# A latent output product with four units of seven products in place of three, and the residual's loads ten ticks later

## The chip, the core and the metric

The kernel runs on one NeuronCore of a Trainium2 chip. The core has a matrix engine (PE, with PEld for its weight loads), a vector engine (DVE), a scalar engine (ACT), a general engine (POOL) and a synchronisation engine (SP); each works through its own list of instructions in a fixed order. SP and POOL issue the DMAs that bring data from memory; the DMAs of both share the core's 16 DMA engines. The metric is the device time of one execution in microseconds (us), the median of several runs; lower is better.

## The reference

One layer of a decoder with 256 tokens and a model width of 2048: two attention branches (a latent one, A, and a sliding-window one, B), each with a gate, merged and put through W_out, then a gated feed-forward part with a short convolution. The place that matters is the output product of branch A, `o_a @ w_o_mla`, a 256 x 2048 by 2048 x 2048 product:

```python
    o_a = mla_attention(q[..., :MLA_NOPE_DIM], q_rope, kv[..., :MLA_NOPE_DIM], k_rope, kv[..., MLA_NOPE_DIM:])
    o_b = swa_attention(q_s, k_s, v_s, swa_sinks, rel_table)
    g = jax.nn.sigmoid(gates.astype(jnp.float32)).reshape(B, S, N_BRANCHES, D_MODEL)
    merged = g[:, :, 0] * (o_a @ w_o_mla).astype(jnp.float32) + g[:, :, 1] * (o_b @ w_o_swa).astype(jnp.float32)
    return merged.astype(h.dtype) @ w_out
...
        y = hybrid_mixer(h, w_in[l], mla_q_norm[l], mla_w_q_up[l], mla_kv_norm[l], mla_w_kv_up[l],
                         swa_sinks[l], rel_bias_table, w_o_mla[l], w_o_swa[l], w_out[l])
        x = x + rms_norm(y, norm_mix_post[l])
```

## The kernel before

**Products in three passes.** All weights are float32. A chunk of weights (128 x 1024, 512 KB) is loaded into a raw buffer; ACT rounds it to a high part `whi` (line 164), DVE subtracts that from the raw chunk and keeps the rest as a low part `wlo` (line 165). Each product is then three matmuls, high by high, high activations by low weights, and low by high (`mm3`, lines 199 to 201). So a chunk goes through load (SP), cast (ACT), subtraction (DVE), matmuls (PE).

**The A pair.** `a_pair` (line 1079) computes the first 1024 of the 2048 output columns of `o_a @ w_o_mla` with `pair_gemm` (line 274). The inner dimension is cut into eight units of two 128-row blocks. A plain unit ("p", line 288) takes two chunks, each with 4 products, that is 12 matmuls, so 24 in all. A unit of seven products ("s", line 301) is a Strassen-like step on 2 x 2 blocks with 7 products, that is 21 matmuls, but it takes four chunks: row block 2u+1 (2 products), the first half of row block 2u (1 product, a load of 256 KB), and two "parked" chunks `tw{u}_0` and `tw{u}_1` (2 products each) that hold differences of weight blocks. It needs sums of the activations too: `a_sums` (line 1060) makes them on DVE with one cast on ACT (`token_sums`, line 376) into the tiles `as0` (units 0 and 1) and `as1` (units 2 and 3). `A_ORDER` says which unit follows which; the seven-product units are the units 0, 1, 2 ... in turn, the plain ones the rest.

**Parking.** The differences in `tw{u}_*` are made long before, in the attention stage, by `park_sums` (line 238): POOL loads two 512 KB chunks into the single tile `tw{u}_s`, DVE does four subtractions of 128 x 512 (line 253), POOL stores two 512 KB results to memory. One more such job, `tc0` for a later product, comes after them and uses the same single tile.

**Buffers.** `RING = 4` pairs of `whi`/`wlo` and `RAW = 3` raw buffers are used in turn. Within the A pair four more raw buffers are in the rotation: chunk by chunk it goes raw, flex, raw, half of `araw`, raw, flex, other half of `araw` (line 1086), with two flex buffers. A load may be issued only when the DVE subtraction of the chunk that last had its buffer is over, and a cast may start only when PE is done with the chunk four before. After the A pair comes the product for columns 1024 to 1535, an ordinary `gemm` (line 203) of eight chunks, c0 to c7 in what follows, 12 matmuls each, with the raw buffers in the order raw, raw, flex, flex, raw.

**What else runs there.** At the end of the pair's last seven-product unit DVE combines the sums into `uda` (lines 356 to 361), adds the plain part (line 1094) and merges with the gates (lines 1069 and 1070). `late_loads` (line 1026) issues eight SP loads of 256 KB that bring the residual x into `x2_0` and `x2_1`; these tiles lie where `as0` and `as1` were, so they wait for PE's last use of the sums. `w_place` (line 1178) later takes the space of `araw` for two POOL loads of W_out, `mr` (512 KB each, lines 326 and 327): they are issued once the last chunk in `araw` has been subtracted.

**Order.** `at(t, f)` puts a step at a due time in ticks (a unit of either kind is two ticks, a chunk of an ordinary product one). The framework's scheduler makes each engine's final order from that program order and the dependences, so a due time is a wish, and the resulting lists are what counts.

Of the kernel before, what the change touches and what calls it, by code (L numbers as in the profile page):

```python
# [42 lines left out]
def trunk_layer(ctx, tc, x, x_cols_in, conv_cols_in, g_mix_post, g_ffn_post, w_in, w_q, w_kv,  # L43
# [16 lines left out]
    def sb(pl, shape, name, dt=F32, tag=None, bufs=None):  # L60
        return pl.tile(shape, dt, name=name, tag=tag or name, **({"bufs": bufs} if bufs else {}))
# [87 lines left out]
    def turn_flex(kind):  # L149
        flex[0] = kind  # L150
        turn.update(raw=0, w=0)
# [27 lines left out]
    now = [0]  # L179

    def at(t, *fs):
        steps[max(t, now[0])].extend(fs)
# [843 lines left out]
    def late_loads(i):  # L1026

        if i < 4:
            if i == 0:
                gpost.append(sb(p6, [P, D], "gpost", tag="gp"))  # L1030
            pool.dma_start(gpost[0][:, i * 512:(i + 1) * 512], g_mix_post[i * 512:(i + 1) * 512].partition_broadcast(P))
        else:
            t, j = divmod(i - 4, 4)
            nc.sync.dma_start(x2[t][j], x[t * P:(t + 1) * P, j * 512:(j + 1) * 512])
# [44 lines left out]
    def a_pair():  # L1079
        halves = [sb(p6, [P, 1024], f"l{n}1", tag="f" + n, bufs=2) for n in "ab"]  # L1080
        lds = [merge_loads(0), [[x_[:, t * 512:(t + 1) * 512] for x_ in halves] for t in range(NT)]]
        for t in range(NT):
            for x_, src in zip(lds[1][t], (ta_d, yb_d)):
                pool.dma_start(x_, src[1, t])
        gp = sb(p6, [P, D], "araw", tag="gp")
        more_raw[:] = [raw_of, raw_f, raw_of, lambda name: gp[:, 0:1024], raw_of, raw_f, lambda name: gp[:, 1024:2048]]
        c = pair_gemm("a", wo_a, 0, 0, A_ORDER, lambda k, t: (AH(k)[:, t * P:(t + 1) * P], AL(k)[:, t * P:(t + 1) * P]),
                      lambda u: as_[u], 0, ud_place, parked=parked_w)
# [13 lines left out]
    for u in range(NA_):  # L1102
        at(now[0] + 3 * u, lambda u=u: a_sums(u))
    for i in range(4, 12):
        at(now[0] + 20 + 2 * i, lambda i=i: late_loads(i))
    turn_flex("raw")
    a_pair()
    yg_all = [[sb(p6, [P, 1024], f"yg_{t}_{j}", tag="f" + "ab"[t], bufs=2) for j in range(2)] for t in range(NT)]
# [455 lines left out]


RING = 4
A_ORDER = "ppspspsp"
NA_ = A_ORDER.count("s")
GATE_ORDER = "psppspsp"
B_ORDER = "psspsspssp"  # L1570
# [81 lines left out]
```

## Time and profile before

| | |
|---|---|
| median of 3 runs | 1456.21 us (1455.47 to 1457.33) |
| the profiled execution, device time | 1455.35 us |
| its span, first to last instruction | 1453.6 us |
| PE busy in the span | 1443.9 us |
| DVE busy in the span | 1162.5 us |
| ACT busy in the span | 866.5 us |
| mean granted PE clock | 0.998 of full speed |

The profile is one execution. The views show, for each engine, when it was busy, what ended its idle time ("<-" names the releaser), and for a DMA the time from its issue to its landing. "PEclk" in a window is the clock that PE was granted, 1.00 being full speed; "DMA" is the mean busy share of the 16 DMA engines.

### The profile page before, as it was taken

What the parts mean: (1) busy time and instruction counts of PE and PEld (TensorE: products, weight loads), DVE (VectorE), ACT (ScalarE), POOL (GpSimd) and SP (SyncE); (2) the same over time, 40 slices, a digit from 0 to 9 for tenths busy, and PEclk for the clock granted to TensorE, in tenths of its full rate; (3) what the DMA queues carried; (4) which work ended last, traced back from release to release, by engine and by line L of the source; (5) the groups of instructions that cost most, each with busy time, mean ns of one, the idle gap of its engine ahead of it and who ended that gap; (6) DMA issues with size and microseconds to landing.
All of it is one profiled execution on the core that took longest, in us unless ns stands there. A gap on an engine that the chain in (4) does not pass through costs nothing.

```text
span 1453.6 us, 21420 instructions
## 1 busy us (share of the span) xinstructions
PE 1443.9 (99%) x7522; PEld 1233.6 (85%) x7522; DVE 1162.5 (80%) x2034; ACT 866.5 (60%) x1422; POOL 113.6 (8%) x204
## 2 busy tenths in 40 slices
PE   9999999999999999999999999999999999999997
PEld 7888888888898888888888888888888888888886
DVE  7788896766878775888799899876777797986798
ACT  7588864544555655546576565655646565565673
POOL 0012110010000001100000011000000101010000
PEclk9999999999999999999999999999999999999999
DMA  8755376698775759975666898866878888788965
GB/s 301 218 171 163 104 262 193 218 325 292 245 218 175 231 155 321 353 232 177 216 207 212 266 335 302 279 208 213 310 271 268 307 276 291 248 282 275 356 216 208
DMA packets 164744, 359.74 MB, mean 247 GB/s; under 512 B 20843, under 2 KB 32012, under 8 KB 164636
## 3 DMA queue, kind: packets, MB, share of 16 engines
q1 hardware_dynamic: 143296, 282.76, 59.8%
q0 software_dynamic: 21248, 75.56, 15.1%
q8 instruction: 59, 0.97, 0.3%
q14 instruction: 49, 0.40, 0.1%
q10 hardware_dynamic: 92, 0.05, 0.0%
HBM read 323.67 MB, written 34.65 MB: 247 GB/s over the span
## 4 chain that ended last, share of the span: by engine, by line
PE 97%; DVE 1%; ACT 1%; issue 0%; DVEq 0%; ACTq 0%
PE ub L1345 10%; PE ua L1345 10%; PE accg L199 10%; PE accg L201 10%; PE accg L200 10%; PE ub L1349 5%; PE ua L1349 5%; PE cd L200 2%; PE cd L201 2%; PE cd L199 2%; PE cdc L200 1%; PE cdc L199 1%; PE cdc L201 1%; PE mpo L981 1%; PE cdb L200 1%; PE cdb L199 1%
## 5 line engine op out<-in xcount | busy, mean ns | idle before, releaser
L164 ACT CAST whi<-raw 128x1024 fp32r<-128x1024 f32 (+2 forms) x498 | 504.5, 1022 | 374.7 <-PE accg L201 107.6
L165 DVE TENSOR_TENSOR wlo<-raw,whi 128x1024 fp32r<-128x1024 f32 (+2 forms) x498 | 586.1, 1189 | 176.0 <-ACT whi L164 171.4
L199 PE MATMUL accg<-whi,ahl 128*128 128x512 f32 (+1 forms) x416 | 162.8, 391 | 0.0
L201 PE MATMUL accg<-whi,ahl 128*128 128x512 f32 (+1 forms) x416 | 160.7, 386 | 0.0
L200 PE MATMUL accg<-wlo,ahl 128*128 128x512 f32 (+1 forms) x416 | 159.9, 384 | 0.0
L1345 PE MATMUL ub<-ahl,whi 128*128 128x512 f32 x640 | 154.7, 391 | 0.0
L1345 PE MATMUL ua<-ahl,whi 128*128 128x512 f32 x640 | 154.6, 391 | 0.0
L1345 PEld LDWEIGHTS ub<-ahl,whi 128*128 128x128 f32 x640 | 117.5, 188 | 22.8 <-ACT cc L1237 0.2
L1345 PEld LDWEIGHTS ua<-ahl,whi 128*128 128x128 f32 x640 | 117.5, 188 | 22.7
L199 PE MATMUL accg<-whi,bhl 128*128 128x512 f32 x256 | 100.7, 393 | 0.0
L201 PE MATMUL accg<-whi,bhl 128*128 128x512 f32 x256 | 99.9, 390 | 0.0
L200 PE MATMUL accg<-wlo,bhl 128*128 128x512 f32 x256 | 99.8, 390 | 0.0
L201 PEld LDWEIGHTS accg<-whi,ahl 128*128 128x128 f32 x416 | 78.1, 188 | 15.5
L200 PEld LDWEIGHTS accg<-wlo,ahl 128*128 128x128 f32 x416 | 78.2, 188 | 13.2
L199 PEld LDWEIGHTS accg<-whi,ahl 128*128 128x128 f32 x416 | 78.2, 188 | 12.9
L1349 PEld LDWEIGHTS ub<-ahl,wlo 128*128 128x128 f32 x640 | 82.3, 191 | 3.2
L1349 PEld LDWEIGHTS ua<-ahl,wlo 128*128 128x128 f32 x640 | 82.2, 191 | 3.1
L1349 PE MATMUL ua<-ahl,wlo 128*128 128x256 f32 x640 | 83.7, 283 | 0.0
L1349 PE MATMUL ub<-ahl,wlo 128*128 128x256 f32 x640 | 83.3, 283 | 0.0
L201 PEld LDWEIGHTS accg<-whi,bhl 128*128 128x128 f32 x256 | 48.0, 188 | 10.1
L200 PEld LDWEIGHTS accg<-wlo,bhl 128*128 128x128 f32 x256 | 48.1, 188 | 9.7
L199 PEld LDWEIGHTS accg<-whi,bhl 128*128 128x128 f32 x256 | 48.1, 188 | 9.6
(660 smaller groups left out, 2682.7 us busy)
## 6 DMA issues: line engine op xcount, KB each, us to landing
raw<-in_ffn_w_up_dram SPq DMA_DIRECT2D x142, 512.0 KB, 4.8
raw<-in_w_in_dram SPq DMA_DIRECT2D x105, 512.0 KB, 4.6
raw<-in_ffn_w_down_dram SPq DMA_DIRECT2D x66, 512.0 KB, 5.7
xraw<-in_ffn_w_up_dram SPq DMA_DIRECT2D x34, 512.0 KB, 5.1
raw<-in_w_o_swa_dram SPq DMA_DIRECT2D x32, 512.0 KB, 4.8
raw<-in_w_o_mla_dram SPq DMA_DIRECT2D x26, 512.0 KB, 5.9
raw<-in_w_out_dram SPq DMA_DIRECT2D x26, 512.0 KB, 4.6
ta_s<-in_ffn_w_down_dram POOLq DMA_DIRECT2D x24, 512.0 KB, 6.2
```

The source lines that it names most:

```text
L164: act.copy(hi[:, a:b], raw[:, a:b])
L165: vec.tensor_tensor(lo[:, a:b], raw[:, a:b], hi[:, a:b].bitcast(F32), op=ALU.subtract)
L199: pe.matmul(o, ah, bh, start=start, stop=False)
L200: pe.matmul(o, ah, bl, start=False, stop=False)
L201: pe.matmul(o, al, bh, start=False, stop=stop)
L981: pe.matmul(o, w(t), p_[:, c], start=n == 0, stop=n == 5)
L1345: pe.matmul(acc[i], hi[:, c], hn[p][:, j * 512:(j + 1) * 512], start=p + j == 0, stop=stop)
L1349: pe.matmul(acc[i][:, 0:256], lo[:, c], hn[p][:, j * 512:j * 512 + 256], start=False, stop=False)
```

## The change

The string that orders the units of the A pair gets four seven-product units and four plain ones, in another sequence, and the residual's loads are due ten ticks later. `NA_`, the count of "s" in the string, sets how many activation sums are made and how many weight differences are parked, so both grow from three to four, and `tc0` is parked seven ticks later.

```diff
     for u in range(NA_):
         at(now[0] + 3 * u, lambda u=u: a_sums(u))
     for i in range(4, 12):
-        at(now[0] + 20 + 2 * i, lambda i=i: late_loads(i))
+        at(now[0] + 30 + 2 * i, lambda i=i: late_loads(i))
...
-A_ORDER = "ppspspsp"
+A_ORDER = "pspspssp"
 NA_ = A_ORDER.count("s")
```

How the lists of instructions move, at three places.

SP's loads at the end of the A pair, before. `tw2_*` are the parked chunks of the last seven-product unit, the next two rows the last plain unit's chunks, and raw390, raw392, raw394 and raw396 are c0, c1, c2 and c3 of the product that follows.

```order
L172 DMA raw382_6248<-tw2_0_3736 128x1024
L172 DMA raw384_6260<-tw2_1_3737 128x1024
L172 DMA araw_5963<-in_w_o_mla_dram 128x1024
L172 DMA raw388_6293<-in_w_o_mla_dram 128x1024
L143 DMA raw394_6369<-in_w_o_mla_dram 128x2x512
L143 DMA raw390_6327<-in_w_o_mla_dram 128x2x512
L1034 DMA x2_0_5938<-in_x_dram 128x512 x2
L143 DMA raw392_6348<-in_w_o_mla_dram 128x2x512
L1034 DMA x2_0_5938<-in_x_dram 128x512
L143 DMA raw396_6390<-in_w_o_mla_dram 128x2x512
```

The same place now: c0, c1, c2 and c3 are raw394, raw396, raw398 and raw400.

```order
L1034 DMA x2_0_5949<-in_x_dram 128x512
L172 DMA araw_5974<-tw3_0_3738 128x1024
L172 DMA raw388_6287<-tw3_1_3739 128x1024
L172 DMA raw390_6300<-in_w_o_mla_dram 128x1024
L172 DMA raw392_6321<-in_w_o_mla_dram 128x1024
L1034 DMA x2_0_5949<-in_x_dram 128x512 x3
L143 DMA raw394_6355<-in_w_o_mla_dram 128x2x512
L143 DMA raw398_6397<-in_w_o_mla_dram 128x2x512
L143 DMA raw396_6376<-in_w_o_mla_dram 128x2x512
L143 DMA raw400_6418<-in_w_o_mla_dram 128x2x512
```

The residual's loads stand ahead of c0 now (one of them inside the pair) or, four of them, behind c6, and no longer between c0 and c3. The last chunk in `araw` is a parked chunk, three chunks before the pair's end, where it was the last but one.

DVE at the end of the pair, now. wlo397 is the subtraction of c1 and wlo399 that of c2; between them stand the sums and merges of the pair.

```order
L165 TENSOR_TENSOR wlo393_6324<-raw392_6321,whi393_6323 128x1024
L356 TENSOR_TENSOR uda_6299<-uda_6299,qa_3_6027 128x512
L165 TENSOR_TENSOR wlo395_6358<-raw394_6355,whi395_6357 128x1024
L357 TENSOR_TENSOR uda_6299<-uda_6299,qa_2_6026 128x512
L165 TENSOR_TENSOR wlo397_6379<-raw396_6376,whi397_6378 128x1024
L360 TENSOR_TENSOR uda_6299<-uda_6299,qa_1_6025 128x512
L361 TENSOR_TENSOR uda_6299<-uda_6299,qa_1_6025 128x512
L1094 TENSOR_TENSOR uda_6299<-uda_6299,ca_0_5975 128x512
L1094 TENSOR_TENSOR uda_6299<-uda_6299,ca_2_5977 128x512
L1069 SCALAR_TENSOR_TENSOR lta0_0_5962<-lta0_0_5962,uda_6299 128x512
L1070 TENSOR_TENSOR lta0_0_5962<-lta0_0_5962,lyb0_0_5963 128x512
L165 TENSOR_TENSOR wlo399_6400<-raw398_6397,whi399_6399 128x1024
```

This sequence is the one of before, operation for operation; the rows of lines 1069 and 1070 come twice each, for the two halves of the tokens.

DVE at the start of the pair, before. wlo351 and wlo353 are the pair's third and fourth chunk.

```order
L384 TENSOR_TENSOR at2_6123<-at2_6123 128x128
L418 TENSOR_TENSOR as1_6122<-at2_6123,as1_6122 128x512
L165 TENSOR_TENSOR wlo351_6016<-raw350_6013,whi351_6015 128x1024
L165 TENSOR_TENSOR wlo353_6033<-araw_5963,whi353_6032 128x1024
L165 TENSOR_TENSOR wlo355_6063<-raw354_6060,whi355_6062 128x1024
```

And now:

```order
L384 TENSOR_TENSOR at2_6148<-at2_6148 128x128
L418 TENSOR_TENSOR as1_6147<-at2_6148,as1_6147 128x512
L378 TENSOR_TENSOR at3_6203<-bhl3_4159 128x512
L165 TENSOR_TENSOR wlo351_6031<-raw350_6028,whi351_6030 128x1024
L381 TENSOR_TENSOR at3_6203<-at3_6203 128x128
L382 TENSOR_TENSOR at3_6203<-at3_6203 128x128
L383 TENSOR_TENSOR at3_6203<-at3_6203 128x128
L384 TENSOR_TENSOR at3_6203<-at3_6203 128x128
L165 TENSOR_TENSOR wlo353_6042<-araw_5974,whi353_6041 128x512
L418 TENSOR_TENSOR as1_6147<-at3_6203,as1_6147 128x512
L165 TENSOR_TENSOR wlo355_6051<-raw354_6048,whi355_6050 128x1024
```

The six operations on `at3` are the activation sums of the fourth unit; the fourth chunk is now the half load of the first seven-product unit.

## The prediction, made before the changed kernel was run

> **What bounds the kernel now.** I read the page first (busy times, chain), then the windows around the A pair, then the engines' timelines at its end.
>
> ```profile
> span 1453.6 us, 21420 instructions
> PE 1443.9 (99%) x7522; PEld 1233.6 (85%) x7522; DVE 1162.5 (80%) x2034; ACT 866.5 (60%) x1422; POOL 113.6 (8%) x204
> PE 97%; DVE 1%; ACT 1%; issue 0%; DVEq 0%; ACTq 0%
> ...
> core 0: us, PE busy (x) PEld busy (x) DVE busy (x) ACT busy (x) POOL busy (x), PEclk, DMA share, GB/s
> 551.47:592.97 41.50, 41.50 (x185) 34.36 (x184) 26.14 (x27) 22.77 (x25) 3.77 (x7) 1.00 0.94 336
> 588.00:606.00 18.00, 18.00 (x83) 14.91 (x82) 17.61 (x24) 6.31 (x6) 2.14 (x4) 1.00 1.01 362
> ```
>
> PE is the bound: 97% of the chain that ended last, and inside the A pair (551.47 to 592.97) it is busy the whole 41.50 us. There is no PE stall to win back there; a change can gain the PE time it removes and lose whatever wait it puts into PE. Two resources stand close behind. In 588 to 606 the DMA engines are full (share 1.01, 362 GB/s), and DVE is busy 17.61 of 18.00 us.
>
> **The matmuls removed.**
>
> ```profile
> 551.47 0.39 PE L199 MATMUL ca<-whi,bhl 128*128 128x512 f32 x1
> ...
> 592.95 0.39 PE L199 MATMUL accg<-whi,bhl 128*128 128x512 f32 x1
> ...
> 598.62 0.39 PE L200 MATMUL accg<-wlo,bhl 128*128 128x512 f32 x1
> ```
>
> The first row opens the pair, the second the product behind it, so 5 x 24 + 3 x 21 = 183 matmuls take 41.48 us, 0.227 us each. Four plain and four seven-product units are 4 x 24 + 4 x 21 = 180: three matmuls fewer, -0.68 us. That is the whole gain, 0.05% of the time. What follows runs earlier by that: the pair ends at 592.27.
>
> **The work added off PE.** A seven-product unit casts and subtracts 3.5 chunks, a plain one 2: 1.5 x 1.22 = 1.8 us more on DVE (1.22 us is a subtraction in the DVE rows below), 1.5 x 1.06 = 1.6 us on ACT. Inside the pair DVE is busy 26.14 and ACT 22.77 of 41.50 us, so idle time covers both. The fourth unit's sums cost DVE and ACT:
>
> ```profile
> L417 ACT CAST as<-at x3: 620/622/627, 535.6 to 548.7; 128x512 fp32r<-128x512 f32 x3
> L418 DVE TENSOR_TENSOR as<-at,as x3: 683/685/693, 536.8 to 549.4; 128x512 fp32r<-128x512 f32 x3
> L384 DVE TENSOR_TENSOR at<-at x2: 291/292/292, 542.2 to 548.4; 128x128 f32<-128x128 f32 x2
> L253 DVE TENSOR_TENSOR tc_s<-tc_s x16: 660/686/689, 494.2 to 1309.7; 128x512 f32<-128x512 f32 x16
> 520.00:540.00 20.00, 20.00 (x121) 17.50 (x120) 12.98 (x23) 11.71 (x21) 1.09 (x2) 1.00 0.60 185
> ```
>
> Two wide ones of 0.69 and four narrow ones of 0.29 are 2.5 us on DVE, and 0.62 us on ACT, at the pair's start where DVE has that idle time; the sums are first needed by the fourth unit, over 25 us later. Parking adds four subtractions of 0.69 us (2.7 us on DVE) and four 512 KB transfers to the attention stage; the window 520 to 540, where the shifted `tc0` job lands, has 7 us of idle DVE and DMA engines at 0.60. I put all of this at nothing. Without that cover the DVE part would cost at most its sum, 7 us; I see no place where PE waits for it.
>
> **The loads.** The pair now loads 22 chunks' worth (4 x 2 + 4 x 3.5) in place of 20.5, 0.79 MB more, and the last two seven-product units stand side by side. The question is which load becomes late, and the tightest is c1, the second chunk of the product behind the pair.
>
> ```profile
> 577.59 1.51 SPq L143 DMA_DIRECT2D raw<-in_w_o_mla_dram  x2
> 579.15 1.05 SPq L1034 DMA_DIRECT2D x<-in_x_dram  x2
> 582.57 0.38 SPq L143 DMA_DIRECT2D raw<-in_w_o_mla_dram  x1
> 583.00 0.47 SPq L1034 DMA_DIRECT2D x<-in_x_dram  x1
> 585.29 0.38 SPq L143 DMA_DIRECT2D raw<-in_w_o_mla_dram  x1
> 585.71 1.64 SPq L1034 DMA_DIRECT2D x<-in_x_dram  x2
> 588.09 3.83 SPq L143 DMA_DIRECT2D raw<-in_w_o_mla_dram  x3
> ...
> 586.92 0.53 POOL L326 DMA_DIRECT2D mr<-in_w_out_dram  x1 [29.22 <-DMA raw<-in_w_o_mla_dram]
> 587.45 0.53 POOL L327 DMA_DIRECT2D mr<-in_w_out_dram  x1
> ...
> 584.31 1.06 ACT L164 CAST whi<-araw 128x1024 fp32r<-128x1024 f32 x1 [0.30 <-PE ca L201]
> 587.97 1.06 ACT L164 CAST whi<-raw 128x1024 fp32r<-128x1024 f32 x1 [0.22 <-DMA raw<-in_w_o_mla_dram]
> ...
> 581.32 1.23 DVE L165 TENSOR_TENSOR wlo<-raw,whi 128x1024 fp32r<-128x1024 f32 x1 [2.02 <-ACT whi L164]
> 584.04 1.22 DVE L165 TENSOR_TENSOR wlo<-raw,whi 128x1024 fp32r<-128x1024 f32 x1 [1.49 <-ACT whi L164]
> 590.31 1.22 DVE L165 TENSOR_TENSOR wlo<-raw,whi 128x1024 fp32r<-128x1024 f32 x1
> 596.24 1.22 DVE L165 TENSOR_TENSOR wlo<-raw,whi 128x1024 fp32r<-128x1024 f32 x1
> ```
>
> Before, c1 is issued at 582.57, the moment the subtraction of 581.32 (chunk 19 of 22, `tw2_0`) frees its raw buffer; that is 10.4 us ahead of the pair's end. Its cast, at 587.97, is already the first one in the pair that waits for a landing (0.22 us). Now the pair has 24 chunks. Counting the raw buffers through the rotation of seven, c0 inherits chunk 19's and c1 chunk 22's, which is the last parked chunk, `tw3_1`. Before, the last parked chunk's subtraction (584.04, ending 585.26) is over 2.25 us ahead of the end of its unit, since its cast starts when PE leaves the chunk four before. The same chunk of the fourth unit: that unit ends 24 matmuls ahead of the pair's end, at 586.83, so c1 is issued at about 584.6, 7.7 us ahead of the end.
>
> How late may it land? c1's subtraction starts at 590.31 and c2's, behind eight `uda` and merge operations, ends at 597.46: 7.15 us without idle time. PE first reads c2's low part at 598.62, now at 597.94. So c1's subtraction must start by 590.8, its cast by 589.7, and it must have landed by 589.6: 5.0 us after its issue. Every further microsecond is one of PE stall.
>
> ```profile
> L143 SPq DMA_DIRECT2D raw<-in_w_o_mla_dram x1: 379/379/379, 582.6 to 582.6; - x1
> DMA to landing us min/median/max: 5.3/5.3/5.3
> ...
> L143 SPq DMA_DIRECT2D raw<-in_w_o_mla_dram x1: 379/379/379, 588.1 to 588.1; - x1
> DMA to landing us min/median/max: 8.9/8.9/8.9
> ...
> L172 SPq DMA_DIRECT2D araw<-in_w_o_mla_dram x1: 332/332/332, 575.1 to 575.1; - x1
> DMA to landing us min/median/max: 4.4/4.4/4.4
> ```
>
> Such a load took 4.4 us at 575.1, 5.3 us as c1, and 8.9 us as c4 at 588.1, behind `mr` and four others. What stands ahead of c1 now: c0 (chunk 19 is now the first of the fourth unit, subtracted by about 581.2), c2 a little after it, and the two `mr` loads, which follow the last `araw` chunk and so move from 586.92 to about 583.5. That is 2.1 MB within 3.4 us. Between c1 before (1.6 MB in the 5 us ahead of it, 5.3 us) and c4 (2.4 MB, 8.9 us) this interpolates to 7.6 us. The other way: 2.6 MB with c1 itself at 362 GB/s from 581.2 is 588.4, and 2.9 us of fixed time (4.4 us less 0.52 MB at that rate) makes 591.3, 6.7 us. I take 7.2 us: landing at 591.8, a stall of 2.2 us. The bounds are 4.4 us (no stall) and 9.6 us (c4's time and half a `mr` load more), a stall of 4.6 us.
>
> The other end of the weighing is the page "DMA: Bandwidth & Descriptors" of the Trainium skill, "Anatomy of one DMA": a fixed 2.0 us and the bytes at 436 GB/s, 3.2 us for 512 KB. By it c1 lands at 587.8 and the sum is -0.68 us. No load around the pair's end landed that fast; the quickest quoted took 4.4 us.
>
> c2 itself has its buffer from chunk 20, early enough. The residual's loads wait for PE's last read of the sums: `x2_0` in the pair for the second unit, which ends by then (about 571), and `x2_1` behind c6 for a unit long over; x2 is needed after 720. The ten ticks cost nothing and take 0.8 MB out of the way of c1 to c3.
>
> **Sum.** -0.68 + 2.2 = +1.5 us. The profiled execution took 1455.35 us (span 1453.6 and 1.75 around it) and would take 1456.9; it lies 0.86 us under the median of the runs, so for the median I forecast 1456.21 + 1.5 = 1457.7 us.
>
> **The rivals.**
>
> *In time.* c1 lands within 5.0 us: -0.68 us, 1455.5. For it: the x loads are out of the way, and 5.3 us was enough before. Against it: `mr` comes earlier and issue is 2.7 us later relative to the end.
>
> *Far too late.* c1 needs 8.6 us or more. The point from which it decides is a landing after 593.2, a stall over 3.6 us: then c1's own use stalls as well as c2's. At 8.9 to 9.6 us the stall is 3.9 to 4.6 us, +3.2 to +3.9 us, 1459.4 to 1460.1. For it: c4 behind the same `mr` pair, and a DMA share of 1.01. A long stall has a second price:
>
> ```profile
> 1445.30 0.28 PE L201 MATMUL zb<-whi,ghl 128*128 128x256 f32 x1
> 1446.00:1450.00 4.00, 0.00 (x0) 0.00 (x0) 3.67 (x12) 0.81 (x3) 0.00 (x0) 0.79 0.17 62
> 1450.00:1453.00 3.00, 0.00 (x0) 0.00 (x0) 0.44 (x1) 0.00 (x0) 0.00 (x0) 0.50 0.72 266
> ```
>
> After the last matmul the granted clock falls to 0.50, at about 1448.3 by the mean of 0.79, 3.0 us after that matmul began. A stall of 3 us or more could do the same and run some 3 us of matmuls at half speed: another 1.5 us, 1461 to 1462. The Trainium skill, "TensorE: Matmul & The Clock Gate", "The HAM clock gate", states the same with a free-running window of about 3.4 us, so a stall of 2.2 us should keep the clock; no run here shows a stall inside the kernel.
>
> *The first half of the pair.* The first seven-product unit is a unit earlier and DMA is busy anyway; the 0.79 MB more are 2.2 us at 362 GB/s, at most that much stall: +1.5 us alone, +3.7 us with the forecast stall, 1459.9. Against it: no cast in the pair waited for a landing before c1's.
>
> **How the numbers follow.** Forecast (c1 late by 0.2 to 3.5 us) 0.49, its own range 1455.7 to 1459.1; in time 0.11; far too late 0.27; first half with the forecast stall 0.10; nothing in the profile gives a gain beyond 0.68 us, and I leave 0.03 for one I can't see. A measurement of this kernel can tell about 0.2%, 2.9 us, from no change, so the first two are "same", 0.60; slower by more has 0.27 + 0.10 = 0.37, faster 0.03. The range, 1455.2 to 1460.4, leaves out the clock's fall, the worst of the far-too-late case and the unseen gain.
>
> **What would show it.** Right: PE 183 to 180 matmuls in the pair, a pause of PE of 1 to 3 us just ahead of c2's second matmul, c1's cast idle on a landing at about 591 to 592, c1 issued near 584.6 and `mr` near 583.5, and DVE idle ahead of c1's subtraction. Wrong: PE without a pause there (in time), a pause before 592, or a granted clock under 1.00 behind it.

## The result and the profile after

| | before | changed |
|---|---|---|
| median of 8 runs each | 1456.24 us (1455.32 to 1457.47) | 1460.84 us (1458.19 to 1464.62) |
| ratio, 95% interval | 1 | 1.0032 (1.0022 to 1.0041) |
| profiled execution, device time | 1455.35 us | 1458.19 us |
| its span | 1453.6 us | 1456.3 us |

The changed kernel is slower by 0.32%, 4.6 us, where 1.5 us were forecast, and the time lies 0.4 us above the top of the range. The profiled execution is the shortest of the eight, so it shows less of the loss (2.8 us) than the median has.

First the page of the changed kernel (span, busy times, chain of waits) and two windows, the A pair and the stretch behind it, with the columns as before.

```profile
span 1456.3 us, 21447 instructions
PE 1443.4 (99%) x7519; PEld 1232.6 (85%) x7519; DVE 1169.7 (80%) x2046; ACT 867.9 (60%) x1425; POOL 115.7 (8%) x208
...
PE 93%; DVE 2%; ACT 2%; DMA 1%; issue 1%; SPq 0%; DVEq 0%; ACTq 0%
...
551.47:592.27 40.80, 40.80 (x182) 33.78 (x181) 27.38 (x30) 22.90 (x26) 3.77 (x7) 1.00 0.96 356
588.00:606.00 18.00, 14.83 (x66) 11.96 (x65) 14.05 (x19) 6.32 (x7) 1.71 (x4) 1.00 0.92 311
```

The pair runs without a hole and is three matmuls shorter. Behind it, in 588 to 606, PE loses 3.17 of its 18 us. The timeline of PE shows where, and the rows of ACT, DVE, POOL and SP show why (time in us, duration, engine, line; in brackets the idle time before and what ended it; the last row is the landing time of the load above it).

```profile
551.44 0.39 PE L199 MATMUL ca<-whi,bhl 128*128 128x512 f32 x1
...
592.02 0.39 PE L201 MATMUL ca<-whi,bhl 128*128 128x512 f32 x1
592.24 0.39 PE L199 MATMUL accg<-whi,bhl 128*128 128x512 f32 x1
592.47 0.39 PE L200 MATMUL accg<-wlo,bhl 128*128 128x512 f32 x1
592.70 0.39 PE L201 MATMUL accg<-whi,bhl 128*128 128x512 f32 x1
596.25 0.50 PE L199 MATMUL accg<-whi,bhl 128*128 128x512 f32 x1 [3.17 <-DVE uda L361]
...
592.70 2.94 ACT L164 CAST whi<-raw 128x1024 fp32r<-128x1024 f32 x3 [4.49 <-DMA raw<-in_w_o_mla_dram]
...
589.38 0.68 DVE L357 TENSOR_TENSOR uda<-uda,qa 128x512 f32<-128x512 f32 x1
593.78 1.23 DVE L165 TENSOR_TENSOR wlo<-raw,whi 128x1024 fp32r<-128x1024 f32 x1 [3.71 <-ACT whi L164]
594.92 0.68 DVE L360 TENSOR_TENSOR uda<-uda,qa 128x512 f32<-128x512 f32 x1
595.52 0.68 DVE L361 TENSOR_TENSOR uda<-uda,qa 128x512 f32<-128x512 f32 x1
...
583.49 0.53 POOL L326 DMA_DIRECT2D mr<-in_w_out_dram  x1 [26.91 <-DMA x<-in_x_dram]
584.01 0.53 POOL L327 DMA_DIRECT2D mr<-in_w_out_dram  x1
...
L143 SPq DMA_DIRECT2D raw<-in_w_o_mla_dram x1: 367/367/367, 584.6 to 584.6; - x1
DMA to landing us min/median/max: 8.0/8.0/8.0
```

Read from the bottom: c1 is issued at 584.6 behind the two `mr` loads and takes 8.0 us, so it lands at 592.6. Its cast starts at 592.70 after 4.49 us of idle ACT; its subtraction starts at 593.78 after 3.71 us of idle DVE. Behind that subtraction in DVE's list stand lines 360 and 361, although they need nothing of c1. Line 361 is the last reader of one of the four result banks of the seven-product units, and the product behind the pair takes over just that bank for its second half of the tokens. So PE does three matmuls of c0, at 592.24 to 592.70, and then waits for line 361. The next one starts at 596.25 in place of 592.92, 3.33 us late. The granted clock stays at 1.00 in this execution. The sum is closed: -0.68 for the matmuls and +3.33 for the pause make +2.65, and the span grew by 2.7 us.

From landing to PE it is 596.25 - 592.60 = 3.65 us (cast, subtraction, lines 360 and 361), and PE wants the bank 0.68 us behind the pair's end: c1 has to land 2.98 us ahead of the pair's end (from the unrounded times), and every later microsecond is one of pause.

### The profile page after: what moved, and what is told of

Same layout as the page of the kernel before. It is cut to its first block, busy times and chain, and to the rows that moved or that the text cites. A ratio compares the mean times of both kernels' runs of the same rounds, so it can differ in the third digit from the quotient of the medians.

```text
span 1456.3 us, 21447 instructions
## 1 busy us (share of the span) xinstructions
PE 1443.4 (99%) x7519; PEld 1232.6 (85%) x7519; DVE 1169.7 (80%) x2046; ACT 867.9 (60%) x1425; POOL 115.7 (8%) x208
## 4 chain that ended last, share of the span: by engine, by line
PE 93%; DVE 2%; ACT 2%; DMA 1%; issue 1%; SPq 0%; DVEq 0%; ACTq 0%
PE ua L1345 10%; PE ub L1345 10%; PE accg L199 10%; PE accg L201 10%; PE accg L200 9%; PE ua L1349 5%; PE ub L1349 5%; PE cd L200 2%; PE cd L199 2%; PE cd L201 2%; PE cdc L200 1%; PE cdc L199 1%; PE cdc L201 1%; DVE wlo L165 1%; DMA raw<-in_w_in_dram 1%; PE cdb L200 1%
## 5 line engine op out<-in xcount | busy, mean ns | idle before, releaser
L201 PEld LDWEIGHTS accg<-whi,bhl 128*128 128x128 f32 x256 | 48.0, 188 | 10.1
```

The costliest lines, as they stand in the source:

```text
L201: pe.matmul(o, al, bh, start=False, stop=stop)
```

## The experiments

Times of different executions are shifted against each other by up to 1.6 us at this place, so the table counts from the pair's end (the first `accg` matmul of each trace). "Needed pause" is the landing time plus 2.98 us; that number comes from the first profile of the changed kernel, so its row agrees by construction and the other rows test it. The ratio is against the executions of the kernel before in the same series (21 to 28 of them, medians 1456.43 to 1456.60), and it need not agree with the quotient of two medians.

| kernel | median us | ratio to before, 95% interval | c1 issued | c1 took | c1 landed | needed pause | PE pause |
|---|---|---|---|---|---|---|---|
| before | 1456.24 | 1 | -10.4 | 5.3 | -5.1 | 0 | 0 |
| changed | 1460.84 | 1.0032 (1.0022 to 1.0041) | -7.66 | 8.0 | +0.36 | 3.34 | 3.33 |
| changed, again | 1460.94 | 1.0030 (1.0019 to 1.0041) | -7.66 | 7.7 | 0.0 | 2.97 | 2.97 |
| shift alone | 1456.54 | 1.0003 (0.9995 to 1.0012) | -10.4 | 5.8 | -4.5 | 0 | 0 |
| order alone | 1460.12 | 1.0029 (1.0017 to 1.0040) | -7.66 | 8.3 | +0.64 | 3.62 | 3.61 |
| c1 in chunk 20's buffer | 1456.18 | 1.0004 (0.9994 to 1.0015) | -10.5 | 6.7 | -3.8 | 0 | 0 |
| the same, again | 1456.01 | 0.9996 (0.9987 to 1.0005) | -10.4 | 6.3 | -4.2 | 0 | 0 |
| banks exchanged | 1461.29 | 1.0036 (1.0024 to 1.0049) | -7.66 | 8.0 | +0.36 | | 3.06, at 598.5 |
| side by side early | 1457.48 | 1.0003 (0.9994 to 1.0012) | -7.66 | 5.7 | -1.95 | 1.03 | 1.03 |
| three units, side by side last | 1458.63 | 1.0012 (1.0002 to 1.0022) | -9.0 | 6.9 | -2.2 | 0.81 | 0.81 |
| `mr` later | 1457.23 | 1.0002 (0.9992 to 1.0011) | -7.66 | 5.3 | -2.3 | 0.64 | 0.64 |
| both remedies | 1455.88 | 0.9994 (0.9985 to 1.0003) | -13.6 | 7.1 | -6.5 | 0 | 0 |

### Which half of the change

```diff
-A_ORDER = "pspspssp"
+A_ORDER = "ppspspsp"
```

> The changed kernel with the old order of units (three units of seven products); only the residual's loads stay ten ticks later. Theory (c1 is late because of the order): PE does not pause near 593, and the time is that of before, 1455.5 to 1457. Rival (the later loads share in the loss, since four of them now collide with the loads behind c6): 1458 or more, with a PE pause after 600.

The later loads of x alone gave 1.0003 (0.9995 to 1.0012), and PE has no pause behind the pair. The opposite, the new order with the old due time:

```diff
-        at(now[0] + 30 + 2 * i, lambda i=i: late_loads(i))
+        at(now[0] + 20 + 2 * i, lambda i=i: late_loads(i))
```

> The changed kernel with the residual's loads at their old due time; only the order of units is new. Theory (the loads of x are traffic beside c1, and the later due time helps): the PE pause at 593 is at least as long as in the changed kernel's profile (3.3 us), time 1459 to 1463. Rival (the due time causes the pause): no pause, 1455.5 to 1456.5.

1.0029, with a pause of 3.61 us. So the loss is the order's. The later due time saves at most a few tenths of a microsecond of c1's landing (8.0 against 8.3 us, one execution each).

### The buffer

```diff
-        turn.update(raw=0)
+        turn.update(raw=1)
```

> The changed kernel, but the raw buffers behind the pair are taken in turn from the second one on, so c1 gets the flex buffer of chunk 20 and c2 that of chunk 23. Theory (the buffer of chunk 22 makes c1 late): c1 is issued at about 581.8 and lands at about 588.4, the PE pause at 593 is gone, and the three matmuls fewer show: 1455.3 to 1456.0, 0.9968 of the changed kernel. Second possibility inside the theory: c2, now issued at about 586 and landing at about 594, pauses PE near 598 by up to 1 us: 1456 to 1457. Rival (the added traffic or the work on DVE makes the loss, whatever buffer c1 has): 1458 or more.

With this one digit c1 gets the buffer of chunk 20, is issued 10.5 us ahead of the pair's end and lands 3.8 us ahead of it, and the pause is gone; DVE and ACT do the same work as in the changed kernel. The median is 1456.18 us, 4.7 us below the changed kernel's. Its profiled execution, though, was one of two long ones of twelve (1461.72 and 1462.96): its ACT timeline, the list of PE's waits and the windows show a wait elsewhere, 1350 to 1364, in the feed-forward part (a row of the list gives the total, the count and the longest, in us).

```profile
1350.71 1.05 ACT L164 CAST whi<-raw 128x1024 fp32r<-128x1024 f32 x1 [4.01 <-DMA raw<-tb]
...
PE cdb L199 <- ACT whi L164: 1.2, 1, 1.2
PE cdb L200 <- DVE wlo L165: 0.8, 1, 0.8
PE qdb L200 <- DVE wlo L165: 0.8, 1, 0.8
...
1352.00:1356.00 4.00, 2.04 (x7) 1.05 (x6) 2.32 (x5) 2.06 (x6) 0.00 (x0) 1.00 0.95 376
1356.00:1362.00 6.00, 5.24 (x13) 3.95 (x13) 6.00 (x9) 5.03 (x7) 0.00 (x0) 0.51 0.69 214
1362.00:1364.00 2.00, 2.00 (x9) 1.59 (x8) 2.00 (x2) 1.24 (x2) 0.00 (x0) 0.77 1.01 345
```

A cast waits 4.01 us for a load there, PE pauses three times, for 0.8, 1.2 and 0.8 us, and then has a clock of 0.51. Whether this edit makes that wait likelier was asked by running it once more.

> The changed kernel with c1 in the buffer of chunk 20, once more. Theory (its two long executions came from a wait near 1353 that this change does not touch): most executions 1455 to 1456.6, median 1455.5 to 1456.3, no PE pause near 593. Rival (the change makes the wait near 1353 likelier): a quarter or more of the executions above 1458.5.

None of eleven executions was above 1457.27, and the median was 1456.01. The profiled execution of another variant (`mr` later, below) has a wait of the same kind: the cast waits 4.17 us for a load, and PE pauses near 1358 for 0.6 and 0.8 us. The kernel before had an execution as long (1462.53, one of 28, with a mean granted clock of 0.996 against 0.998 or 0.999 in the others), but it was not profiled. Whether the kernel before has this wait too is therefore not shown, and its cause was not looked for.

### Which wait is the first

```diff
-            q1, q5, q7, q6 = q
+            q1, q5, q7, q6 = q if name != "a" else q[2:] + q[:2]
```

The edit stands at both places that name the banks.

> The changed kernel, but the four sums of the seven-product units change places in the result memory of PE: the bank that the product behind the pair takes second is then freed by the operation of line 356 or 357, ahead of c1's subtraction on DVE, instead of line 361 behind it. Theory A (the forecast's step: c1 is late, and the wait for a bank is only the first of two that hang on it): the pause at 593 goes, and one of about the same length (2.5 to 3.3 us) comes ahead of c2's second matmul near 598; time within 1 us of the changed kernel, 1459 to 1461.5. Theory B (the bank alone is what costs): no pause over 1 us, 1455.5 to 1457.

Theory A held. The two `accg` banks now come free with lines 356 and 357, ahead of c1's subtraction, and c0 and c1 run through. The pause comes at c2's low part:

```profile
598.23 0.39 PE L199 MATMUL accg<-whi,bhl 128*128 128x512 f32 x1
601.52 0.50 PE L200 MATMUL accg<-wlo,bhl 128*128 128x512 f32 x1 [2.90 <-DVE wlo L165]
...
600.25 1.22 DVE L165 TENSOR_TENSOR wlo<-raw,whi 128x1024 fp32r<-128x1024 f32 x1
```

c2 landed long before; its subtraction is late only because it stands behind c1's and eight other operations on DVE. This is the wait that the prediction named, and it is the second of two. Taking the first away wins nothing.

### Why c1 is late: the count and the neighbours

```diff
-A_ORDER = "pspspssp"
+A_ORDER = "psspspsp"
```

> Four units of seven products as in the changed kernel, but the two that stand side by side come early in the pair and the last two stand a plain unit apart, as before. Theory (the number of chunks, 24, hands c1 the buffer of the last parked chunk, wherever the others stand): c1 is issued at about 584.6 again, and the PE pause near 593 is 2.5 to 4 us, time 1458 to 1462. Rival (the two units side by side at the end make the loads late): no pause over 0.5 us, 1455.3 to 1456.2.

Half of the theory fell, and the time, 1457.48 us, lies between what theory and rival gave. c1 is issued exactly as late as in the changed kernel, 7.66 us ahead of the end: the count of 24 chunks sets that. But it lands after 5.7 us, and the pause is 1.03 us. SP and POOL in this kernel, and SP in the changed one:

```profile
579.62 0.98 SPq L143 DMA_DIRECT2D raw<-in_w_o_mla_dram  x2
580.65 0.93 SPq L1034 DMA_DIRECT2D x<-in_x_dram  x2
586.19 4.89 SPq L143 DMA_DIRECT2D raw<-in_w_o_mla_dram  x4
...
583.73 0.53 POOL L326 DMA_DIRECT2D mr<-in_w_out_dram  x1 [24.18 <-DVE wlo L165]
```

```profile
577.48 1.38 SPq L1034 DMA_DIRECT2D x<-in_x_dram  x3
581.18 14.21 SPq L143 DMA_DIRECT2D raw<-in_w_o_mla_dram  x7
```

The pair ends at 593.85 here and at 592.24 in the changed kernel. So c0 and c2 are issued 14.2 and 13.6 us ahead of the end here, 11.1 and 10.5 there; `mr` starts 10.1 us ahead here and 8.75 there. A buffer comes free a cast and a subtraction after PE is done with the chunk four before. c0's buffer comes from chunk 19, the first of the last seven-product unit, and the chunk four before is chunk 15. With a plain unit between the last two seven-product units, 30 matmuls lie between the end of chunk 15 and the start of chunk 19; with the two side by side it is 15. The 15 matmuls are 3.4 us, near the 3.1 us by which c0 goes out earlier. With the two side by side, c0, c2, both `mr` loads and c1 go out within 3.4 us, and c1 has 2.1 MB just ahead of it. With 24 chunks the late issue comes from the count, the crowd ahead of it from the neighbours.

```diff
-A_ORDER = "pspspssp"
+A_ORDER = "pppspssp"
```

> Three units of seven products, the last two side by side at the end of the pair. Theory (the number of chunks is that of before, so c1 inherits the buffer of the third chunk from the last plain unit, free early): c1 is issued near 582, no PE pause near 593, time 1456 to 1457. Rival (two side by side): a PE pause of 1 us or more, 1457.5 or more.

Here the theory failed and the rival was nearer. With three units c1's buffer comes from the same chunk as before, but that chunk too is freed later when the units are neighbours: c1 is issued 9.0 us ahead, not 10.4, and takes 6.9 us. The pause is 0.81 us in the profiled execution (1457.04 us) and the median, 1458.63, suggests longer ones in others.

### The crowd ahead

```diff
         both = sb(p6, [P, D], f"mr{i}", tag="gp")
+        for k in range(2):
+            vec.tensor_copy(both[:, k * 1024:k * 1024 + 1], mth[0][:, 0:1].bitcast(F32))
```

> The changed kernel, but the two loads of mr wait for the first transposed columns behind the pair (two copies of 128 x 1 on DVE stand ahead of them), so they are issued near 610 and no longer just ahead of c1. Theory (1 MB of mr ahead of c1 is what stretched its landing from 5.3 to 8.0 us): c1 is still issued at about 584.6 and lands after 5 to 6.3 us, at 589.6 to 590.9; the PE pause shrinks to 0.3 to 1.6 us, the granted clock stays at 1.00, time 1455.8 to 1457.5. Rival (the late issue alone, whatever stands ahead): landing after 7.5 us or more, pause 2.5 us or more, 1458 or more.

```profile
L143 SPq DMA_DIRECT2D raw<-in_w_o_mla_dram x1: 368/368/368, 585.9 to 585.9; - x1
DMA to landing us min/median/max: 5.3/5.3/5.3
...
594.86 0.50 PE L199 MATMUL accg<-whi,bhl 128*128 128x512 f32 x1 [0.48 <-DVE uda L361]
...
PE cw L199 <- DVE lta L1069: 1.7, 1, 1.7
```

With `mr` out of the way c1, issued at the same place, takes 5.3 us in place of 8.0: the 1 MB of `mr` is worth 2.4 to 2.7 us of landing against the two profiles of the changed kernel. The pause behind the pair shrinks to 0.64 us. The median falls to 1457.23 us. The profiled execution is the longest of the ten (1461.62 us): it has a wait of 1.7 us at the start of the product with W_out (last row) and the two pauses near 1358 named above. Whether the 1.7 us is a price of this edit is not shown, because the kernel with both remedies, which leaves `mr` where it was, waits 1.1 us at the same place.

### The rest of the median, and both remedies

> The changed kernel once more, unchanged, for a second profiled execution. Theory (its median lies 2.65 us above its profiled execution because in most executions the pause is longer than the 3.2 us there and the granted clock falls behind it): pause of 3 to 5 us near 593, and in a slower execution PEclk of 0.5 for several us behind it. Rival (the rest of the median's loss lies elsewhere in the span): the pause as in the first profile, and a second pause later.

The pause, 2.97 us, is no longer than in the first profile, so that half of the theory fell; the granted clock is what the first profile lacks. The pause and the windows behind it of this second execution, then of the kernel with the order alone, and the windows of that with the banks exchanged (its pause is shown above):

```profile
597.11 0.50 PE L199 MATMUL accg<-whi,bhl 128*128 128x512 f32 x1 [2.81 <-DVE uda L361]
...
597.00:598.00 1.00, 0.90 (x3) 0.71 (x4) 1.00 (x3) 0.00 (x0) 0.00 (x0) 0.89 0.77 193
598.00:600.00 2.00, 2.00 (x6) 1.61 (x5) 2.00 (x5) 0.00 (x0) 0.00 (x0) 0.50 0.93 201
600.00:602.00 2.00, 2.00 (x7) 1.56 (x7) 2.00 (x4) 1.05 (x1) 1.08 (x2) 0.70 0.95 291
```

```profile
597.02 0.79 PE L199 MATMUL accg<-whi,bhl 128*128 128x512 f32 x1 [3.45 <-DVE uda L361]
...
596.00:598.00 2.00, 0.98 (x2) 0.83 (x3) 2.00 (x4) 0.40 (x1) 0.00 (x0) 0.59 0.44 118
598.00:600.00 2.00, 2.00 (x6) 1.57 (x5) 2.00 (x5) 0.00 (x0) 0.00 (x0) 0.50 0.84 217
600.00:602.00 2.00, 2.00 (x6) 1.52 (x6) 2.00 (x3) 0.74 (x1) 1.08 (x2) 0.50 0.91 293
602.00:604.00 2.00, 2.00 (x8) 1.57 (x7) 2.00 (x4) 0.31 (x1) 0.00 (x0) 0.71 1.06 368
```

```profile
600.00:602.00 2.00, 0.48 (x2) 0.43 (x3) 2.00 (x4) 0.00 (x0) 1.08 (x2) 0.98 0.94 328
602.00:604.00 2.00, 2.00 (x7) 1.54 (x6) 2.00 (x4) 0.00 (x0) 0.00 (x0) 0.50 1.03 363
604.00:606.00 2.00, 2.00 (x8) 1.59 (x7) 2.00 (x4) 0.06 (x1) 0.10 (x1) 0.66 0.85 303
```

A window of length w with mean clock m was at 0.50 for 2 x (1 - m) x w. That makes 0.22 + 2.00 + 1.20 = 3.4 us in the first fence, 1.64 + 4.00 + 1.16 = 6.8 us in the second, and 0.08 + 2.00 + 1.36 = 3.4 us in the third. About half of that is lost: 1.7 us, 3.1 us (0.7 us of it still lay in the pause) and 1.7 us. So the changed kernel costs -0.68 + 3.0 to 3.3 us for the pause and, where the clock falls (in one of its two profiles and in those of both its close relatives), 1.7 us or more besides: +2.3 to +2.7 without, +4.0 to +4.3 with it. The median difference of 4.6 us fits executions in which the clock falls. This execution, 1461.26 us, also lost about 1.2 us ahead of the pair, which ended at 593.46, not 592.24.

The executions without a profile have a mean granted clock on record, in steps of 0.001. 3.4 us at half clock take 0.0012 from it. It is 0.997 or less in 12 of the 15 executions of the changed kernel, and in 1 of 74 of the kernel before (the others have 0.998 or 0.999). So the clock fell in most executions of the changed kernel; where in the span it fell, only the profiles show. A value of 0.998 does not rule a fall out: the profiled execution with the banks exchanged has it, with 3.4 us at 0.50. The changed kernel has it in its first profile, where the clock did not fall, and in two long executions (1462.33 and 1462.65 us), for which it stays open. How long the pause was in the executions without a profile stays open too.

The two remedies together, the neighbours early and c1 in the buffer of chunk 20:

```diff
-        turn.update(raw=0)
+        turn.update(raw=1)
...
-A_ORDER = "pspspssp"
+A_ORDER = "psspspsp"
```

> Both remedies together: four units of seven products with the side-by-side pair early, and c1 in the buffer of chunk 20. Theory (nothing of the loss is left, and the three matmuls fewer show): c1 lands over 5 us ahead of the pair's end, no PE pause near 593, granted clock 1.00 there, time 1455.3 to 1456.2, 0.2 to 1 us below before (0.9993 to 0.9999). Rival (the added conversions, sums and parking cost something elsewhere): 1456.5 to 1458.

```profile
592.28 0.39 PE L199 MATMUL accg<-whi,bhl 128*128 128x512 f32 x1
592.51 0.39 PE L200 MATMUL accg<-wlo,bhl 128*128 128x512 f32 x1
592.74 0.39 PE L201 MATMUL accg<-whi,bhl 128*128 128x512 f32 x1
592.96 0.39 PE L199 MATMUL accg<-whi,bhl 128*128 128x512 f32 x1
...
588.00:606.00 18.00, 18.00 (x83) 14.90 (x82) 17.99 (x24) 6.82 (x8) 2.15 (x4) 1.00 0.99 346
...
PE cw L199 <- DVE lta L1069: 1.1, 1, 1.1
```

No pause behind the pair, PE busy all of 588 to 606. The median is 1455.88 against 1456.60 for before in the same series, -0.72 us, close to what the three matmuls are worth (-0.68). The ratio of 0.9994 (0.9985 to 1.0003) doesn't settle a gain that small, and the profiled execution also has a wait of 1.1 us at the start of the product with W_out (last row), which the kernel before did not have in its profiled execution. So the agreement with -0.68 may be chance; the wait was not followed up.

## Why the prediction was wrong, point by point

- **PE bounds, and only the matmuls can be won:** right. The pair takes 592.24 - 551.44 = 40.80 us against 41.48, -0.68 as forecast, and no PE stall in it, so the rival "The first half of the pair" did not come. The best variant of the new count has a median 0.72 us below before, a gain that its interval does not settle.
- **The added conversions, sums and parking cost nothing:** right for the pair. With c1's buffer exchanged all of that work is still there, PE has no wait in the pair or behind it up to 606, and the ratios are 1.0004 and 0.9996; their intervals, 0.9987 to 1.0015, would hide a cost of some 2 us.
- **Which load becomes late, when, and behind what:** right. c1 was forecast to be issued at 584.6 behind `mr` at 583.5; it was at 584.59, behind `mr` at 583.49.
- **How long c1 takes:** 7.2 us taken, 7.7 to 8.3 measured in the four executions (of three kernels) that issue it behind the same crowd. Of the two ways of reckoning, the interpolation between c1 and c4 of the trace before (7.6) was the better one, and the mean with the bandwidth sum (6.7) pulled it down. The -0.68 and the time of issue were right, this term was too small by 0.8 us in the first profile. The 3.2 us that the prediction sets beside these by the Trainium skill is no bound for c1: the formula in the section named there is for transfers that the general engine issues, and SP issues c1; the shortest c1 measured took 5.3 us.
- **What c1's lateness holds up first:** the step that failed. The prediction followed c1's subtraction to the next subtraction behind it, c2's, and to the matmul that needs it, so it allowed a landing up to 2.67 us ahead of the pair's end. Two of the operations between, lines 360 and 361, free a result bank that PE takes up three matmuls into c0; the limit is 2.98 us. The exchange of banks showed both: without the first wait the second comes, 3.06 us long. In time the oversight is worth 0.3 us; the place of the pause, at 592.9 in place of 598, was wrong by almost two chunks.
- **The clock stays at 1.00:** wrong in most executions, by the clocks on record, and in time the largest part of the miss: 1.7 us each time that it falls, a term that the forecast put at nothing. The prediction let a stall of 3 us or more cost 1.5 us by the clock, but only as part of the rival "far too late" (0.27, 1461 to 1462 us). The median is there in all but 0.2 us. The rival's condition, a landing after 593.2 and a stall over 3.6 us, was wrong: the clock fell behind a pause of 2.97 us, with c1 landing as the pair ended.
- **The residual's loads ten ticks later cost nothing:** right, 1.0003 alone.

In sum +1.5 was forecast: -0.68 + 2.2. The profiled execution has -0.68 + 3.33, where 0.8 of the 1.1 us more is c1's landing and 0.3 the earlier limit. The other 1.8 us between it (+2.8) and the median (+4.6) holds, in most executions, a fall of the clock, which costs some 1.7 us; what the pause and the rest of the span add in each is open. The path that failed (the bank) is thus what set the place of the pause, and the size of the miss came mostly from the clock and from c1's landing.

## What to carry to other kernels

When a load may become late, follow every instruction that stands behind its first user in that engine's list, not only those that read its data: what they free (a bank, a buffer) may be wanted first. A ring of buffers ties a load to whichever chunk used the buffer last, so a change in the number of chunks can hand the next stage's most urgent load the last buffer to come free; a different start of the turn can undo it. And a forecast pause of 2 to 3 us of PE, in one piece or in several close together, should be priced with the clock behind it, because the uncertainty of a DMA's landing is enough to reach it.

## What the runs showed of the hardware

PE's granted clock fell to 0.50 behind pauses with 2.81, 2.90 and 3.45 us of idle time and did not behind one of 3.17 us, so the length of the pause alone doesn't decide. The stretches at 0.50 were 3.4, 3.4 and 6.8 us. It fell too, for 6.8 us by the windows from 1356 to 1364, behind the three pauses of 0.8, 1.2 and 0.8 us in the kernel with c1 in chunk 20's buffer, so no single long pause is needed; two pauses of 0.6 and 0.8 us in the kernel with `mr` later left it at 1.00. The page "TensorE: Matmul & The Clock Gate" of the Trainium skill, "The HAM clock gate", states a free-running window of about 3.4 us and the fall after one idle window. The lengths agree, and so does a fall that depends on where the pause lies; that a whole window must be idle does not, since two of the single pauses were shorter than one.

c1, a load of 512 KB issued 7.66 us ahead of the pair's end, took 5.3 us without, and 7.7 to 8.3 us with, two more of 512 KB issued by another engine some 1 us ahead of it. They delay it by about what their own transfer takes, 1.05 MB at 373 GB/s (the rate of 588 to 592) being 2.8 us: loads that POOL issues cost those of SP their time.

```profile
588.00:592.00 4.00, 4.00 (x19) 3.32 (x18) 1.82 (x2) 0.21 (x1) 0.00 (x0) 1.00 1.02 373
```
